# A down projection written as Strassen's seven products, in a fused mixer and SwiGLU layer

## Chip, core and metric

One Trainium2 chip, one of its cores. The metric is the device time of one execution in microseconds (us). The kernel is a whole decoder layer: four token mixers, their shared output projection, a layer norm, a SwiGLU channel mixer and a second layer norm. The change lies in the channel mixer.

## The reference

1024 tokens, model width 1024, D_FF = 2816 (22 tiles of 128), everything in float32. What bears on the change, after the mixers and the first layer norm have made x, and with sh2, sc2 and g2 the modulation of the sequence:

```python
h = x * (1 + sc2) + sh2
f = (silu(h @ w_gate) * (h @ w_up)) @ w_down
out = layer_norm(ALPHA * x + (1 + g2) * f, ln2_g, ln2_b)
```

w_gate and w_up are 1024 x 2816, w_down is 2816 x 1024.

## The kernel before

Float32 precision comes from splitting: every operand x is stored as a pair, hi = x rounded to the matmul's input type (ACT, L80) and lo = x - hi (DVE, L81), and a product is three matmuls, hi*hi, hi*lo and lo*hi (`passes`, L130 to L132). Pairs lie in tiles that go round (`pair_tile`); raw operands come by DMA into four `raw` tiles, issued by SP in program order; `tmp` is a ring of three 4 KB wide tiles. PSUM has six banks `mm` and two `sm`. The order of instructions on each engine is set by a scheduler from the order of the program, except where `in_order` holds it to program order.

**Gate and up.** For each j from 0 to 10, `strassen(j)` makes the two row tiles 2j and 2j+1 of silu(gate) * up for all tokens. It does this by five products of 24 matmuls on PE, `s1`, `s4`, `s2`, `s3` and `22`, over sums of weights that `a_ops(j)` forms (L725) and sums of activations that were formed once; two further products come from elsewhere, one loaded as `p1`. After each product DVE takes it out of PSUM, in two halves m of 128x512: L757 after `s1`, L761 after `s4`, L767 after `s2`, L774 after `s3`, L778 after `22`. `s4` goes on in the two banks that L757 reads. L781 is the multiplication by up, and L782 stores the finished tile to `act_d` in DRAM, from POOL's queue; a store at L770 writes the second half of the other tile before. `ada(38 + j)` beside it computes the modulation for the second half, and `spread(mod[40:48])` turns it into a row by a scatter through DRAM (`rowa_d`, L470).

**Down.** `down_ops` (L787) loads per row tile f a 128x512 half of act_d and the 128x1024 rows of w_down, and splits both. `down_mm` adds, for token half c, four blocks t of 128 tokens and two column halves h, the three passes into eight banks: 22 x 2 x 4 x 2 x 3 = 1056 matmuls of 128x512, 24 per row tile and half. w_down is loaded and split twice, once for each token half. The table `FB` puts the last few row tiles together so that the blocks t end one after the other, and then `res2` (L829, with L833 and L834) adds the residual to each and `ln2` (L837) normalizes it: statistics by L500 and L503, an inverse root on POOL (L397 to L415), L841, L845 and the store to the output (L846).

Of the kernel before, what the change touches and what calls it, by code (L numbers as in the profile page):

```python
# [50 lines left out]
def trunk(ctx: ExitStack, tc: tile.TileContext, A, out):  # L51
# [39 lines left out]
    def pair_tile():  # L91
        n = sum(b for _, _, b in pairs)
        i = cnt[0] % n
        cnt[0] += 1
        for pl, tg, b in pairs:
            if i < b:
                return pl.tile([P, 2, 1024], F32R, name="pr", tag=f"{tg}{i}", bufs=1)
            i -= b
# [390 lines left out]
    act_d = dr.tile([FT, P, T], F32, name="act_d")  # L489
    KORD = (6, 7, 2, 3, 0, 1, 4, 5)  # L490
# [247 lines left out]
    def strassen(j):  # L738


        ao = a_ops(j)
        w = next(ao)
# [27 lines left out]
        G.dma_start(act_d[2 * j][:, CH:], c12[0])  # L770
# [11 lines left out]
        G.dma_start(act_d[2 * j + 1], hi[0])  # L782

    FB = tuple(tuple((f, f + 1) for f in range(n)) + ((n, 22),) for n in (19, 15))
    dn = {0: {}, 1: {}}

    def down_ops(c, n):  # L787
        b0, b1 = FB[c][n]
        w, act = {}, {}
        more = sl.tile([P, 4, 2, 1024], F32R, name="wd", tag="ha") if b1 - b0 > 3 or c == 1 and n == 0 else None  # L790
        if c == 1 and n == 0:
            dn["first"] = more
        for f in range(b0, b1):
            a = raw_p.tile([P, 1024], F32, name="raw", tag="raw", bufs=4)
            SP.dma_start(a[:, :CH], act_d[f][:, cs(c)])
            act[f] = acts[(c * FT + f) % 8]
            split(act[f][:, 0], act[f][:, 1], a[:, :CH])
            if c == 1 and n < 4:
                w[f] = dn["first"][:, n]
            elif f < b1 - 3:  # L800
                w[f] = more[:, f - b0]
            else:
                w[f] = pair_tile()
            split(w[f][:, 0], w[f][:, 1], raw(A["w_down"][f]))
        dn[c][n] = w, act

    def down_mm(c, n, o):
        (b0, b1), (w, act) = FB[c][n], dn[c][n]
        for t in range(4):
            tt = slice(t * P, (t + 1) * P)  # L810
            if n == 0:
                for h in range(2):
                    o[t, h] = mm() if t < 3 else sm()
            todo = [(f, h) for f in range(b0, b1) for h in range(2)]
            if c == 1 and t == 3 and b1 == FT:
                todo.sort(key=lambda x: x[1])
            for f, h in todo:
# [11 lines left out]
    def res2(o, t, r, x1):  # L829

        for h in range(2):
            hs = slice(h * 512, (h + 1) * 512)
            V.tensor_tensor(out=r[:, hs], in0=o[t, h], in1=g2row[:, hs], op=MUL)  # L833
            V.tensor_tensor(out=r[:, hs], in0=r[:, hs], in1=x1[:, hs], op=ADD)  # L834
            yield

    def ln2(c, t, r, res=None):  # L837

        tok = c * 4 + t
        rs, nm = yield from norm_stats(r, res)  # L840
# [132 lines left out]
    with tc.issue_after(ln_end[0]), tc.issue_after(ln_end[1]), in_order(ON_PE):  # L973
# [50 lines left out]
        run(st)  # L1024
        room = sl.tile([P, 8, 1024], F32, name="room", tag="ha")
        for j in range(1, FT // 2):
            run(strassen(j))
            if j > 1 and j < 10:
                ada(38 + j)

# [4 lines left out]
    ag = row_of("ln1_g_row", sl, "m_up", ALPHA)  # L1035
    ab = row_of("ln1_b_row", sl, "m_zch", ALPHA)
    acts = hb_tiles("acts")
    o0, o1 = {}, {}
    with in_order(ON_PE):
        last = len(FB[0]) - 1  # L1040
        for n in range(last + 1):
            down_ops(0, n)
            if n == last - 1:
                x1 = [keep_x1(0, t) for t in range(4)]
            if n == last:
                for i in range(4):
                    down_ops(1, i)
            down_mm(0, n, o0)
        rr = [yp.tile([P, 1024], F32, name="r2", tag=f"y{4 + t}") for t in range(4)]
        for t in range(4):  # L1050
            run(res2(o0, t, rr[t], x1[t]))
        for n in range(len(FB[1])):
            if n > 3:
                down_ops(1, n)
            down_mm(1, n, o1)
            if 3 < n < 8:
                run(ln2(0, n - 4, rr[n - 4]))
            if n == 8:
                x1 = [keep_x1(1, t) for t in range(4)]
    rr = [tmp() for t in range(3)] + [raw_p.tile([P, 1024], F32, name="r2", tag="raw", bufs=4)]  # L1060
    ln = [ln2(1, t, rr[t], res2(o1, t, rr[t], x1[t])) for t in range(4)]
    with in_order(ON_DVE):
        for t in range(4):
            run(ln[t], 2)
            if t == 2:
# [360 lines left out]
```

## Time and profile before

| | |
|---|---|
| time, median of 3 runs (lowest to highest) | 1039.09 us (1038.07 to 1041.19) |
| the profiled execution's own time | 1037.87 us |
| its span in the trace | 1036.1 us |
| PE busy | 980.8 us, 95% |
| DVE busy | 737.7 us, 71% |
| ACT busy | 344.5 us, 33% |
| POOL busy | 184.4 us, 18% |
| moved by DMA | 177.75 MB, 172 GB/s over the span |

The page gives, for each engine, the busy time, its share of the span and the number of instructions. Busy time is an average over stages, so it says what fills the whole, and not what a stage waits for; for that the windows (busy time by stretch, with the granted clock of PE and the busy share of the DMA engines) and the timelines are read. In a timeline a row is: start, duration, engine, line and operation, output<-inputs, shape, and in square brackets the idle time of the engine just before and what ended it. PE is TensorE, DVE VectorE, ACT ScalarE, POOL GpSimd, SP SyncE. A matmul's duration in a row is longer than the distance to the next, since matmuls overlap in the pipeline.

### The profile page before, as it was taken

The page shows a single profiled execution, that of the slowest core. Times are in us where ns is not written, and L with a number is a line of the kernel's source. Part 1 is how long each engine was busy: PE and PEld are TensorE (multiplying, and loading weights), DVE is VectorE, ACT ScalarE, POOL GpSimd, SP SyncE. Part 2 cuts the span into 40 slices and gives each one's busy share as a digit, 9 for nine tenths or more (in the row PEclk, how much of TensorE's full clock was granted, in tenths as well). Part 3 has the DMA queues.
Part 4 walks back from the last instruction along what each step waited for, and adds up shares of the span by engine and source line. Part 5 has one row for each costly group of instructions (what it writes and reads, how often), then busy time and mean ns, then how long its engine had stood idle before and what let it go on. Part 6 is the DMA issues. An engine that isn't in the chain of part 4 may idle for free.

```text
span 1036.1 us, 12527 instructions
## 1 busy us (share of the span) xinstructions
PE 980.8 (95%) x4480; PEld 799.9 (77%) x4480; DVE 737.7 (71%) x1184; ACT 344.5 (33%) x537; POOL 184.4 (18%) x515
## 2 busy tenths in 40 slices
PE   8949999898989989899899999999999999999995
PEld 7837777676887868687688888887888888888884
DVE  5858998888669952757898777776568433776656
ACT  4632211424464351374322222222233333312500
POOL 7990000300351020541000000000000000050013
PEclk9979999998999999899999999999999999999998
DMA  8833212686454363597954344443247534654601
GB/s 314 321 112 104 53 41 90 219 225 223 158 204 172 147 237 104 188 316 267 347 175 159 138 147 152 146 148 111 82 149 284 174 136 142 232 185 148 228 21 61
DMA packets 65694, 177.75 MB, mean 172 GB/s; under 512 B 11040, under 2 KB 17216, under 8 KB 65632
## 3 DMA queue, kind: packets, MB, share of 16 engines
q1 hardware_dynamic: 57760, 149.17, 42.7%
q0 software_dynamic: 7872, 27.79, 6.7%
q8 instruction: 35, 0.57, 0.2%
q14 instruction: 27, 0.22, 0.1%
HBM read 142.26 MB, written 34.09 MB: 170 GB/s over the span
## 4 chain that ended last, share of the span: by engine, by line
PE 60%; DVE 10%; DMA 5%; POOL 4%; ACT 3%; issue 2%; SPq 0%; DVEq 0%; POOLq 0%; ACTq 0%
PE mm L132 18%; PE mm L130 18%; PE mm L131 17%; PE sm L130 2%; PE sm L132 2%; PE sm L131 2%; DMA raw<-in_w_ada_dram 2%; DMA raw<-h_d 2%; DVE pr L81 1%; DVE acc L429 1%; DMA raw<-in_w_gate_dram 1%; DVE raw L168 1%; ACT tmp L598 1%; DVE lst L500 1%; POOL rs_a L397 1%
## 5 line engine op out<-in xcount | busy, mean ns | idle before, releaser
L81 DVE TENSOR_TENSOR pr<-raw,pr 128x1024 fp32r<-128x1024 f32 (+1 forms) x139 | 138.1, 1003 | 77.7 <-ACT pr L80 77.4
L80 ACT CAST pr<-raw 128x1024 fp32r<-128x1024 f32 (+1 forms) x139 | 119.2, 878 | 179.4 <-PE sm L132 68.4
L130 PE MATMUL mm<-bop,pr 128*128 128x512 f32 x264 | 103.2, 391 | 4.2 <-DVE c L767 3.5
L131 PE MATMUL mm<-bop,pr 128*128 128x512 f32 x264 | 102.8, 389 | 0.0
L132 PE MATMUL mm<-bop,pr 128*128 128x512 f32 x264 | 102.7, 389 | 0.0
L130 PE MATMUL mm<-h,pr 128*128 128x512 f32 (+1 forms) x208 | 77.0, 370 | 8.0 <-ACT p L643 7.1
L429 DVE SCALAR_TENSOR_TENSOR acc<-up,pack,acc 128x512 f32<-128x512 f32 x120 | 84.3, 742 | 0.1
L130 PE MATMUL mm<-pr,acts 128*128 128x512 f32 x216 | 84.0, 389 | 0.0
L131 PE MATMUL mm<-pr,acts 128*128 128x512 f32 x216 | 84.0, 389 | 0.0
L132 PE MATMUL mm<-pr,acts 128*128 128x512 f32 x216 | 84.0, 389 | 0.0
L132 PE MATMUL mm<-h,pr 128*128 128x512 f32 (+1 forms) x208 | 75.4, 362 | 2.9 <-DVE pr L81 2.9
L131 PE MATMUL mm<-h,pr 128*128 128x512 f32 (+1 forms) x208 | 75.2, 361 | 0.0
L132 PE MATMUL mm<-tb,pr 128*128 128x512 f32 x176 | 68.8, 391 | 1.1 <-DVE pr L81 1.0
L130 PE MATMUL mm<-tb,pr 128*128 128x512 f32 x176 | 68.7, 390 | 1.0 <-ACT pr L80 1.0
L131 PE MATMUL mm<-tb,pr 128*128 128x512 f32 x176 | 68.5, 389 | 0.0
L397 POOL TENSOR_SCALAR rs_a<-lmv 128x1 f32<-128x1 f32 x16 | 11.0, 689 | 318.1 <-DVE lmv L503 317.8
L168 DVE SCALAR_TENSOR_TENSOR raw<-raw,cond 128x1024 f32<-128x1024 f32 x48 | 58.1, 1218 | 13.3 <-DMA raw<-in_w_ada_dram 13.2
L80 ACT CAST pr<-room 128x512 fp32r<-128x512 f32 x60 | 34.3, 619 | 87.9 <-PE mm L132 83.9
L130 PEld LDWEIGHTS mm<-bop,pr 128*128 128x128 f32 x264 | 49.6, 188 | 16.4 <-DVE c L767 2.9
L132 PEld LDWEIGHTS mm<-bop,pr 128*128 128x128 f32 x264 | 49.6, 188 | 10.3
L131 PEld LDWEIGHTS mm<-bop,pr 128*128 128x128 f32 x264 | 49.6, 188 | 10.1
L131 PE MATMUL mm<-h_a,pr 128*128 128x512 f32 x104 | 42.7, 410 | 13.7 <-DVE h_a L81 13.5
(311 smaller groups left out, 2182.4 us busy)
## 6 DMA issues: line engine op xcount, KB each, us to landing
raw<-in_w_ada_dram SPq DMA_DIRECT2D x48, 512.0 KB, 4.8
raw<-in_w_down_dram SPq DMA_DIRECT2D x44, 512.0 KB, 3.7
raw<-in_w_gate_dram SPq DMA_DIRECT2D x23, 512.0 KB, 4.7
raw<-in_w_up_dram SPq DMA_DIRECT2D x23, 512.0 KB, 4.2
raw<-act_d SPq DMA_DIRECT2D x44, 256.0 KB, 3.3
raw<-in_w_o_dram SPq DMA_DIRECT2D x16, 512.0 KB, 4.4
p_d<-p POOLq DMA_DIRECT2D x11, 512.0 KB, 2.9
act_d<-tmp POOLq DMA_DIRECT2D x11, 512.0 KB, 2.9
```

What stands on the lines that cost most here:

```text
L80: S.copy(hi, src)
L81: V.tensor_tensor(out=lo, in0=src, in1=hi.bitcast(F32), op=SUB)
L130: PE.matmul(o, wh, xh, start=first, stop=False, skip_group_check=True)
L131: PE.matmul(o, wh, xl, start=False, stop=False, skip_group_check=True)
L132: PE.matmul(o, wl, xh, start=False, stop=last, skip_group_check=True)
L168: V.scalar_tensor_tensor(out=w, in0=w, scalar=1.0, in1=cond, op0=MUL, op1=MUL, accum_out=mod[:, j:j + 1])
L397: G.tensor_scalar(out=a, in0=v, scalar1=EPS, scalar2=None, op0=ADD)
L429: V.scalar_tensor_tensor(out=o, in0=u, scalar=dww[:, i, j:j + 1], in1=o, op0=MUL, op1=ADD)
L500: V.bn_stats(st[:, h], r[:, h * 512:(h + 1) * 512])
L598: S.activation(dst, src, AF.Identity, scale=hA[:, kk:kk + 1], bias=hB[:, kk:kk + 1])
```

## The change

With A the activations (row tiles even or odd, tokens first or second half) and B the weights (rows even or odd, columns first or second half), the four blocks of the result are formed from seven products over 11 pairs of tiles:

1 A11 B11, 2 S1 T1, 3 S2 T2, 4 S3 T3, 5 A22 T4, 6 A12 B21, 7 S4 B22.

- The seven products run over `GR`, six groups of two tile pairs (the last has one), 24 matmuls a group, four banks `oA` or `oB` a product. The second half of the result is built up in `oA` and in SBUF (`r0`, `r1`), with copies by ACT and additions by DVE between products (`S.copy`, `res2`, `more_res`).
- S1 to S4, sums of the activations, are formed by DVE at the end of each `strassen(j)` (L788 to L792 of the change) and stored to `s_d` by POOL (two stores of 512 KB); the first half of one tile is read back for it (`c12[1]`), also from POOL's queue. The first part of the weights' sums for j+1 is issued ahead of this.
- T1 to T4, differences of the weights, are formed beside the products: `t13` makes T1 and T3 of a group during product 1, from three more loads of weights into `tmp` tiles, `t2` and `t34` turn T1 into T2 and T4 in place.
- Loads are now pieces of two tile pairs: 128 x 2 x 512, rows of 2 KB each, where w_down came in rows of 4 KB.
- Three more tiles (`m_up`, `m_zch`, `m_zp`) join the ring of pair tiles. The layer norm of the second half of the tokens ends earlier, that of the first half is now the last.

```diff
-    def strassen(j):
+    def strassen(j, ao=None, w=None):
...
-        G.dma_start(act_d[2 * j][:, CH:], c12[0])
+        G.dma_start(c12[1], act_d[2 * j][:, :CH])
...
         G.dma_start(act_d[2 * j + 1], hi[0])
+        yield
+
+        a11, a21, (a12, a22) = c12[1], c12[0], [hi[0][:, H[c]] for c in range(2)]
+        (s1, s3), (s2, s4) = P1, [hi[1][:, H[c]] for c in range(2)]
+        V.tensor_tensor(out=s1, in0=a21, in1=a22, op=ADD)
+        V.tensor_tensor(out=s2, in0=s1, in1=a11, op=SUB)
+        V.tensor_tensor(out=s3, in0=a11, in1=a21, op=SUB)
+        G.dma_start(s_d[j, 0].rearrange("p a t -> p (a t)"), p1)
+        V.tensor_tensor(out=s4, in0=a12, in1=s2, op=SUB)
+        G.dma_start(s_d[j, 1].rearrange("p a t -> p (a t)"), hi[1])
+    GR = tuple((j, min(j + 2, FT // 2)) for j in range(0, FT // 2, 2))
+    def dn_mm(o, lt, rt, g, t, first, last):
+        n = GR[g][1] - GR[g][0]
+        for j in range(n):
+            ls, rs = slice(j * CH + t * P, j * CH + (t + 1) * P), slice(j * CH, (j + 1) * CH)
+            passes(o[t], (lt[:, 0, ls], lt[:, 1, ls]), (rt[:, 0, rs], rt[:, 1, rs]),
+                   first and g == 0 and j == 0, last and g == len(GR) - 1 and j == n - 1)
+    def dn_product(o, left, right, first, last, also=lambda g: None, room=(None, None)):
+        for g in range(len(GR)):
+            lt, rt = [dn_pair(x(g), None if g else y) for x, y in zip((left, right), room)]
+            for t in range(4):
+                dn_mm(o, lt, rt, g, t, first, last)
+            also(g)
...
+        def t13(g):
+            b12, b11, b22 = (w_rows(g, b, h, tmp()) for b, h in ((0, 1), (0, 0), (1, 1)))
+            V.tensor_tensor(out=kept(g), in0=b12, in1=b11, op=SUB)
+            V.tensor_tensor(out=kept(g, True), in0=b22, in1=b12, op=SUB)
...
+        dn_product(oA, lambda g: act_rows(g, 0, 0), lambda g: w_rows(g, 0, 0), True, False, t13)
+        for t in range(4):
+            S.copy(r0[t][:, H[0]], oA[t])
+        dn_product(oB, lambda g: sum_rows(g, 0, 0), kept, True, False)
...
+        dn_product(oA, lambda g: sum_rows(g, 1, 0), t2, False, False)
...
+        dn_product(oA, lambda g: sum_rows(g, 0, 1), t34, False, False)
...
+        dn_product(oA, lambda g: act_rows(g, 1, 1), kept, False, True)
...
+        dn_product(oA, lambda g: act_rows(g, 1, 0), lambda g: w_rows(g, 1, 0), True, True,
+                   room=[more0[:, i] for i in range(2)])
...
+            ops.append((dn_pair(sum_rows(g, 1, 1), two[0]), dn_pair(w_rows(g, 1, 1), two[1])))
...
+        for t in range(4):
+            for g in range(last, len(GR)):
+                dn_mm(oB, *ops[g], g, t, False, True)
```

The scheduler puts the new work between the old. **DVE, from the end of step j=1 to the beginning of j=2, before** (L781 the multiplication of j=1, L757 the first product of j=2, L725 the weights' sums, L81 the splits; in brackets what the instruction waits for):

```order
L778 TENSOR_TENSOR tmp<-room,mm 128x512 [waits PE_49]
L81 TENSOR_TENSOR pr<-room,pr 128x512 [waits Activation_49]
L781 TENSOR_TENSOR tmp<-tmp 128x1024 [waits DVE_49]
L81 TENSOR_TENSOR pr<-room,pr 128x512 [waits Activation_49]
L757 TENSOR_TENSOR tmp<-room,mm 128x512 [waits DMAHW0_49,DMASW7_49,PE_49]
L725 TENSOR_TENSOR raw<-room,raw 128x512
L725 TENSOR_TENSOR raw<-raw,room 128x512 x2
L757 TENSOR_TENSOR tmp<-room,mm 128x512 [waits DVE_49,PE_49]
```

The same place now (L779 was L778, L782 was L781, L758 was L757; L788 to L792 are S1, S2, S3 and S4):

```order
L779 TENSOR_TENSOR tmp<-room,mm 128x512 [waits PE_49]
L81 TENSOR_TENSOR pr<-room,pr 128x512 [waits Activation_49]
L782 TENSOR_TENSOR tmp<-tmp 128x1024 [waits DVE_49]
L790 TENSOR_TENSOR room<-c_4363 128x512 [waits DMASW2_49]
L788 TENSOR_TENSOR room<-c_4363,tmp 128x512 [waits DVE_49]
L758 TENSOR_TENSOR tmp<-room,mm 128x512 [waits DMAHW0_49,DMASW1_49,PE_49]
L789 TENSOR_TENSOR tmp<-room,c_4363 128x512 [waits DVE_49]
L81 TENSOR_TENSOR pr<-room,pr 128x512 [waits Activation_49]
L792 TENSOR_TENSOR tmp<-tmp 128x512 [waits DVE_49]
L81 TENSOR_TENSOR pr<-room,pr 128x512 [waits Activation_49]
L758 TENSOR_TENSOR tmp<-room,mm 128x512 [waits DMASW3_49,DVE_49]
```

The four sums stand between the multiplication and the second L758, two of them ahead of the first; and the second L758 has a wait for a store from POOL's queue (DMASW3, the store of act_d by the step before, whose tile it writes).

**SP, the loads at the beginning of the down projection, now** (L804 is every load of the seven products; `tmp<-in_w_down_dram` are the loads for T1 and T3, `raw<-s_d` the sums for product 2):

```order
L804 DMA tmp<-in_w_down_dram 128x2x512 [waits DMASW3_49,DMASW7_49,DMASW1_49,DVE_49]
L1076 DMA keep<-in_ln_g_row_dram 128x1024 [waits DMASW4_49,DMASW0_49]
L1076 DMA keep<-in_ln_b_row_dram 128x1024
L804 DMA tmp<-in_w_down_dram 128x2x512 [waits DMAHW6_49,DMASW3_49,DMASW1_49]
L804 DMA tmp<-in_w_down_dram 128x2x512 [waits DMAHW7_49,DMAHW3_49,DVE_49]
L804 DMA raw<-in_w_down_dram 128x512 [waits DMAHW0_49,Activation_49]
L804 DMA raw<-s_d 128x2x512 [waits DMAHW1_49,Activation_49]
L804 DMA tmp<-in_w_down_dram 128x2x512 [waits DMAHW2_49,DVE_49]
L804 DMA tmp<-in_w_down_dram 128x2x512 [waits DMAHW6_49]
L804 DMA raw<-s_d 128x2x512 [waits DMAHW4_49,Activation_49]
L804 DMA raw<-s_d 128x2x512 [waits DMAHW5_49,Activation_49]
```

All of these are new; the queue held only `raw<-act_d` and `raw<-in_w_down_dram` here, in turn. Loads into `tmp` wait for DVE's subtractions and for POOL's stores, and the loads of the operands stand behind them.

## Rows read from the trace of the kernel before

**Rows 1.** The page: busy time, share of the span and instructions of each engine.

```profile
PE 980.8 (95%) x4480; PEld 799.9 (77%) x4480; DVE 737.7 (71%) x1184; ACT 344.5 (33%) x537; POOL 184.4 (18%) x515
```

**Rows 2.** Windows: length, busy PE, PEld, DVE, ACT, POOL; PE's clock, DMA share, GB/s.

```profile
785.00:965.00 180.00, 180.00 (x796) 149.10 (x795) 105.61 (x124) 53.28 (x68) 17.36 (x37) 1.00 0.53 182
508.00:540.00 32.00, 31.01 (x135) 24.83 (x134) 31.58 (x53) 12.77 (x21) 1.08 (x2) 1.00 0.64 237
785.00:797.00 12.00, 12.00 (x55) 9.94 (x54) 10.27 (x11) 3.45 (x5) 0.54 (x1) 1.00 0.97 359
830.00:860.00 30.00, 30.00 (x134) 24.86 (x133) 10.84 (x12) 8.49 (x11) 0.00 (x0) 1.00 0.39 137
595.00:622.00 27.00, 27.00 (x121) 22.37 (x120) 20.35 (x34) 7.41 (x12) 1.09 (x2) 1.00 0.41 146
434.00:438.00 4.00, 4.00 (x11) 3.13 (x10) 1.58 (x3) 3.13 (x10) 2.95 (x10) 0.50 0.32 131
```

**Rows 3.** Timeline of PE: first and last matmul of the down projection.

```profile
785.07 0.39 PE L130 MATMUL mm<-pr,acts 128*128 128x512 f32 x1
...
1024.21 0.39 PE L132 MATMUL sm<-pr,acts 128*128 128x512 f32 x1
```

**Rows 4.** Timeline of DVE at an ordinary handover between two steps.

```profile
675.17 0.69 DVE L778 TENSOR_TENSOR tmp<-room,mm 128x512 f32<-128x512 f32 x1 [1.31 <-PE mm L132]
...
680.61 0.69 DVE L757 TENSOR_TENSOR tmp<-room,mm 128x512 f32<-128x512 f32 x1 [1.72 <-PE mm L132]
```

**Rows 5.** Timelines of DVE and of PE at the first handover, j = 0 to 1.

```profile
512.70 1.22 DVE L781 TENSOR_TENSOR tmp<-tmp 128x1024 f32<-128x1024 f32 x1
513.83 0.68 DVE L81 TENSOR_TENSOR pr<-raw,pr 128x512 fp32r<-128x512 f32 x1
514.43 0.68 DVE L725 TENSOR_TENSOR raw<-raw,room 128x512 f32<-128x512 f32 x1
...
516.97 0.39 PE L130 MATMUL mm<-tb,pr 128*128 128x512 f32 x1
```

**Rows 6.** The store of act_d (L782), all steps; step 7's scatter; PE after it.

```profile
DMA to landing us min/median/max: 2.9/2.9/8.6
rowa_d<-mod SPq DMA_DIRECT2D x1, 4.0 KB, 11.1
719.69 0.47 PE L130 MATMUL mm<-bop,pr 128*128 128x512 f32 x1 [1.04 <-DVE c L767]
```

**Rows 7.** DMA issues from 783 to 800, last row 800 to 860: count, KB, us to landing.

```profile
x<-x_d SPq DMA_DIRECT2D x4, 512.0 KB, 6.3
raw<-in_w_down_dram SPq DMA_DIRECT2D x3, 512.0 KB, 4.6
act_d<-tmp POOLq DMA_DIRECT2D x1, 512.0 KB, 5.7
raw<-in_w_down_dram SPq DMA_DIRECT2D x12, 512.0 KB, 3.3
```

**Rows 8.** Groups of instructions, 785 to 1025: count, busy us, mean ns, idle before.

```profile
L81 DVE TENSOR_TENSOR pr<-raw,pr 128x1024 fp32r<-128x1024 f32 x33 | 40.3, 1220 | 51.9 <-ACT pr L80 51.8
L80 ACT CAST pr<-raw 128x1024 fp32r<-128x1024 f32 x33 | 34.7, 1052 | 64.5 <-PE sm L132 53.2 <-DMA raw<-in_w_down_dram 11.2
```

**Rows 9.** Timeline of DVE after the last matmul.

```profile
1025.17 0.68 DVE L833 TENSOR_TENSOR r<-sm,row 128x512 f32<-128x512 f32 x1
...
1027.58 1.28 DVE L841 SCALAR_TENSOR_TENSOR r<-r,lmv,row 128x1024 f32<-128x1024 f32 x1
...
1031.60 1.41 DVE L845 SCALAR_TENSOR_TENSOR r<-r,lrs,row 128x512 f32<-128x512 f32 x2 [2.73 <-POOL lrs L415]
```

**Rows 10.** Timeline of PE: two matmuls after a long pause, one after a shorter.

```profile
433.29 0.79 PE L130 MATMUL mm<-h,pr 128*128 128x512 f32 x1 [4.19 <-ACT p L643]
...
438.57 0.62 PE L130 MATMUL mm<-h,pr 128*128 128x512 f32 x1
...
501.14 0.50 PE L130 MATMUL mm<-bop,pr 128*128 128x512 f32 x1 [2.46 <-DVE c L767]
```

More of the change, by code (lines that the diff above doesn't have):

```diff
@@ L489, in trunk @@
     act_d = dr.tile([FT, P, T], F32, name="act_d")
+    s_d = dr.tile([FT // 2, 2, P, 2, CH], F32, name="s_d")
     KORD = (6, 7, 2, 3, 0, 1, 4, 5)
@@ L782, in strassen @@
         G.dma_start(act_d[2 * j + 1], hi[0])
[L784 to L805, printed above, removed]
@@ L1034, in trunk @@
     l2b = row_of("ln2_b_row", yp, "rowc")
[L1035 to L1038, printed above, removed]
+    pairs.extend((sl, f"m_{n}", 1) for n in ("up", "zch", "zp"))
     with in_order(ON_PE):
[L1040 to L1049, printed above, removed]
-        for t in range(4):
[L1051 to L1059, printed above, removed]
@@ new lines, in kept @@
+        def kept(g, third=False):
+            lo, hi = GR[g]
+            v = keep[:, 11:12] if third and lo == 10 else (kt3 if third else keep)[:, lo:hi]
+            return v.rearrange("p j t -> p (j t)")
+        ag, ab = (keep[:, 12 + 2 * i:14 + 2 * i].rearrange("p j t -> p (j t)") for i in range(2))
+        for row, name in ((ag, "ln1_g_row"), (ab, "ln1_b_row")):
+            SP.dma_start(row, A[name].to_broadcast([P, 1024]))
+            V.tensor_scalar(out=row, in0=row, scalar1=ALPHA, scalar2=None, op0=MUL)
@@ new lines, in trunk, with more_res @@
+        for t in range(4):
+            res2(r1[t], x1[t], 1, r1[t][:, H[1]])
+            run(ln1_[t], 1)
+        for t in range(4):
+            res2(r1[t], x1[t], 0, oA[t])
+        more0 = sl.tile([P, 2, 2, 1024], F32R, name="wd0", tag="hb0")
+        def more_res(t, h, o):
+            f = sl.tile([P, CH], F32, name="f", tag=f"acc{t % 2}")
+            V.tensor_tensor(out=f, in0=o, in1=g2row[:, H[h]], op=MUL)
+            V.tensor_tensor(out=r0[t][:, H[h]], in0=r0[t][:, H[h]], in1=f, op=ADD)
@@ new lines, in trunk @@
+        dn_product(oA, lambda g: act_rows(g, 1, 0), lambda g: w_rows(g, 1, 0), True, True,
+                   room=[more0[:, i] for i in range(2)])
+        for t in range(2):
+            run(ln1_[t])
+        more = sl.tile([P, 4, 2, 1024], F32R, name="wd", tag="ha")
+        last = len(GR) - 4
+        ops = []
+        for g in range(len(GR)):
+            two = (None, None) if g < len(GR) - 2 else [more[:, 2 * (g - len(GR)) + 4 + i] for i in range(2)]
+            ops.append((dn_pair(sum_rows(g, 1, 1), two[0]), dn_pair(w_rows(g, 1, 1), two[1])))
+            if g < last:
+                for t in range(4):
+                    dn_mm(oB, *ops[g], g, t, False, True)
+            if g in (1, 3):
+                run(ln1_[2 + g // 2])
@@ L1070 @@
+        run(ln0[3])
 class SSM:
```

116 lines of the change are left out of this document (79 added, 37 removed).

## The prediction

> **What bounds the kernel now.** I read the page first, then windows over the stage that is changed, then timelines of its borders, then the DMA view. The page [rows 1] shows TensorE busy for 95% of the span, every other engine below three quarters. The windows [rows 2] narrow that: from 785 to 965 us, which is three quarters of the down projection, PE is busy all the time at a granted clock of 1.00, DVE for 105.6 of 180 us, and the DMA engines for half. So the stage is paid by the matmul: its first starts at 785.07, its 1056th at 1024.21 [rows 3], which is 239.14 us over 1055 intervals, **0.2267 us each**. A matmul removed there gives that back, as long as the others find their operands in time. The gate/up stage ahead of it is also full on PE; its border between two steps j has to be looked at separately, because the change puts vector work into it.
>
> The profiled execution took 1037.87 us (span 1036.1 and 1.8 around it), 1.2 below the median of the three runs, 1039.09. My sum is against 1037.87. A difference of 0.3% (3.1 us) is about what a measurement of this kernel tells from none.
>
> **Part 1, fewer matmuls.** Seven products x 11 tile pairs x 4 row tiles x 3 passes = 924 for 1056. 132 x 0.2267 = **-29.9 us**.
>
> **Part 2, the sums S1 to S4 at the end of each strassen(j).** Four 128x512 additions go into DVE's queue among L781 and the two L757 of the next j (the two order pieces of DVE), and two more stores and a reload into POOL's. Consecutive 512-wide operations start 0.60 us apart (513.83 to 514.43) [rows 5], so four are 2.4 us. TensorE wants the first L757 done before the s4 product overwrites its bank, 24 matmuls = 5.44 us after the last product ends, and the second 2.72 later, at 8.16. At an ordinary handover [rows 4] the last product ended at about 675.15; there the second L757 starts at +5.46, after DVE has idled 1.72 us for PE, as it had 1.31 before L778. With the sums in front they are done at about +4.4 and +7.4: both in time, cost 0. Only the first handover has no slack: from 508 to 540 DVE is busy 31.58 of 32 us [rows 2], and PE's s4 product begins at 516.97 [rows 5], right after L757 ends. The four sums push the end of L757 back by all their time, 4 x 0.60, if the scheduler puts them as in the order pieces: **+2.4** (bounds 0, were DVE to catch up in the 1 us that PE lacks there, and 4).
>
> The second L757 (L758 of the change) gains a wait, for the store of act_d by the step before, because the three `tmp` buffers now go round faster. Everything behind it on DVE waits too: splits of the next operands, then PE. The store takes 2.9 us to land in most steps and 8.6 at worst [rows 6]. It is issued at +2.9; up to a landing of 4.6 us the second L757 is still done at 8.16. The worst case is step 7: the row scatter `rowa_d<-mod`, at the same place in SP's queue before and now, takes 11.1 us, and the store issued meanwhile takes the 8.6. Then L757 is done at 2.9 + 8.6 + 0.7 = 12.2 instead of 8.16, 4.0 us late, of which I take off the pause of 1.04 at 719.69 that, as I read it, the same congestion causes already [rows 6]: **+3.0** (bounds 0, if the scatter lands later, and 4).
>
> **Part 3, T1 to T4, weights' differences.** For each of six groups, product 1 also loads three weight pieces into the three `tmp` buffers, and DVE subtracts twice. SP issues in order (third order piece), so a load waiting for a buffer holds up every load behind it, those of PE's operands too. Count from T, the start of the down projection. The first of these loads needs the buffer of the last act_d store: T + 2.9 + 5.7 [rows 7] = T + 8.6; the last two need the last s_d store, about T + 11, and with the landing of 4.6 [rows 7] and two subtractions the buffers of group 0 are free at T + 19.6. From there a round takes: landing 4.6, two 1024-wide subtractions at 1.22 [rows 8] and a little, one split ahead of them, 1.13 as such operations follow each other (512.70 to 513.83) [rows 5], and 0.5 of issue by my estimate: 8.7 us. PE's round is 24 x 0.2267 = 5.44. Product 2 wants group 4 at T + 29.9 + 4 x 5.44 = T + 51.7. It is there after four rounds but for the second subtraction, and a cast and a split, T + 19.6 + 34.8 - 1.2 + 1.05 + 1.22 = T + 55.5: 3.8 late, and group 5, half as large, adds some 1.2. **+5.** Bounds: nothing, if a landing takes 3.3 us as from 800 to 860 [rows 7], for then the round is 7.4 and group 4 comes at T + 50.1, early; 13 with 6.3 us, the landing of `x<-x_d` in the crowded start [rows 7], for then a round is 10.4, group 4 comes 10.6 late and group 5 adds 2.4. I take the middle, since the stretch is fuller than 830 to 860 (137 GB/s) and emptier than 785 to 797 (359 GB/s at 0.97 share) [rows 2]: 66 pieces of 0.262 MB and two rows, about 17.8 MB, move in 59.8 us, 298 GB/s.
>
> Other work of this stretch costs nothing by itself: DVE's splits, subtractions and residuals there come by the new order to 34 operations of 1.13 and 17 of 0.60 us = 48 of 59.8 us, and ACT's casts (1.05 each [rows 8]) to less. If that cover goes, the first to suffer is the split of the T operand. The pieces are now rows of 2 KB where weights were rows of 4 KB. The rows show no price for this: 830 to 860 carries some of its bytes as 2 KB rows (activations) and moves 137 GB/s at 0.39, 351 per unit of share; 595 to 622, with 4 KB rows only, moves 146 at 0.41, 356 per unit [rows 2]. So 0 here. The Trainium skill, "Perfetto Trace Analysis", section DMA Optimizations, says the contrary, that raising transfers from 2 KB to 4 KB improves throughput; if it held, this stretch would be short of bandwidth, which is rival E. These two rows speak against it.
>
> **Part 4, the end.** Product switches on PE 0.3; operands of product 7 that fall behind the loads of the layer norm 0.7. The last four groups run row tile by row tile, 21 matmuls = 4.76 us each. DVE's work per row tile, by its spacing (2.41 from L833 to L841, then 1.28 and 1.41) [rows 9], is 5.1, a little more than PE's: it comes to end some 2 us behind PE where now L833 at 1025.17 follows the last matmul by 0.6, +1.5. The chain after that is the same length, to L845 at 1031.60 [rows 9] and the store. Together **+2.5** (bounds 0.5 and 4).
>
> **Sum.** -29.9 + 2.4 + 3.0 + 5.0 + 2.5 = -17.0: 1037.87 - 17.0 = **1020.9 us**.
>
> **Rivals.**
> B, all covered: landings stay at 3 us, the T rounds keep ahead of PE and the scatter doesn't meet the store; only the first handover is left. 1037.87 - 29.9 + 2.4 = 1010.4. For it: DVE and DMA are half idle from 785 to 965 [rows 2]. Against: both are at their fullest in products 1 and 2.
> A, the T building sets the pace: landings near 6.3, +13 instead of +5: 1029. For it: at 785 to 797 the DMA is at 0.97 already, without the extra loads [rows 2].
> D, the clock: each pause of TensorE is followed by a slow stretch. Shown once: after the pause of 4.19 before 433.29 it runs 12 matmuls at 0.427 us until 438.57, with 0.50 granted, which costs 12 x 0.2 = 2.4 us; after the 2.46 before 501.14 the first matmul takes 0.50, not 0.79, and from 508 on the clock is 1.00 [rows 2, 10]. Were four pauses in T building and one at step 7 of the first kind, +12: 1033. My pauses are 1 to 4 us long, and mostly nearer the second row. [...]
> C, **slower**: the store of act_d lands later than 4.6 us at every handover, since each step now adds a reload and two stores of 0.5 MB to the same queues; L758 then holds DVE, and PE waits up to 4.0 us at ten handovers: 1020.9 - 3 + 40 = 1058. It decides from 4.6 us on. Against: median 2.9 [rows 6], and 0.41 DMA share at those steps [rows 2].
> E, **slower**: 2 KB rows move at half the rate of the 356 GB/s per unit above, 178; 17.8 MB then take 100 us, not 59.8: +40 in place of 5, 1056. The two rows above nearly rule it out.
> That the change doesn't remove the matmuls is excluded: the order of PE has 132 rows fewer, and both print the same form.
>
> **How the numbers follow.** Forecast 0.48, A 0.22, B 0.16, D 0.08, C 0.04, E 0.02. The predicted time is the forecast's, 1020.9. The range reaches from B with the first handover free (1008) to D with a little more (1034) and leaves out C, E and the tails. Slower by over 0.3% are C and E, 0.05 after rounding; within 0.3% only a much worse A or D, 0.02; faster 0.93.
>
> **What would show it.** In the profile after: 924 matmuls at 0.227 us, no other rate; PE idle of about 2.4 us in step 1 before the s4 product, released by DVE L758; a pause of about 3 at step 8 with `act_d<-tmp` landing at 8 us or more; at 20 to 30 us into product 2 idle time of PE released by the split of `pr<-keep`, 5 us in all, with `tmp<-in_w_down_dram` landing in 4 to 5 us. PE idle at every handover would mean C; a granted clock under 1 after the pauses D; a stretch at 0.97 DMA share under 250 GB/s E; no idle in product 2 B. The prediction is wrong if PE idles outside these places, or the stage is shorter than 924 x 0.2267 = 209.5 us.

## The result, and the profile after

| | before | after |
|---|---|---|
| median (lowest to highest) | 1040.09 us (1038.07 to 1041.19, 4 runs) | 1025.55 us (1024.14 to 1029.23, 4 runs) |
| ratio to before, 95% interval | | 0.987 [0.9844, 0.9895] |
| profiled execution's own time | 1037.87 us | 1024.14 us |
| its span | 1036.1 us | 1022.4 us |

The time predicted was 1020.9, in a range from 1008 to 1034; the profiled execution fell by 13.7 us where the sum had 17.0. The page of the changed kernel, with the line of [rows 1], the chain that ended last (for it the page of before has PE at 60% and POOL at 4%), and DMA's totals:

```profile
span 1022.4 us, 12392 instructions
PE 957.6 (94%) x4348; PEld 777.6 (76%) x4348; DVE 808.0 (79%) x1268; ACT 357.3 (35%) x545; POOL 200.1 (20%) x537
issue 31%; PE 21%; DVE 12%; POOL 9%; DMA 8%; ACT 2%; SPq 0%; POOLq 0%; DVEq 0%; ACTq 0%
HBM read 153.79 MB, written 42.74 MB: 192 GB/s over the span
```

PE has 132 instructions less and 23.2 us less busy time, not the 29.9 of 132 x 0.2267, since part of its matmuls now run slower. About half of that gap lies in the down projection (below); of the rest, eight matmuls 0.43 us apart stand at 498.8 to 501.8, after a pause of 1.93 ahead of the places that the change touches. DVE is up 70 us. In the chain line 31% is "issue", time in which the engine waited for nothing that the profile shows (2% before), so the chain can be followed only in part. So the account is made from PE's own timeline, at the places where the distance between two matmuls is more than 0.2267 us:

```profile
520.42 0.50 PE L130 MATMUL mm<-tb,pr 128*128 128x512 f32 x1 [2.24 <-DVE tmp L758]
562.50 0.47 PE L130 MATMUL mm<-bop,pr 128*128 128x512 f32 x1 [0.97 <-DVE c L768]
717.48 0.47 PE L130 MATMUL mm<-tb,pr 128*128 128x512 f32 x1 [1.87 <-DVE tmp L758]
791.04 0.39 PE L130 MATMUL mm<-pr 128*128 128x512 f32 x1
821.88 0.51 PE L131 MATMUL mm<-pr 128*128 128x512 f32 x1 [0.53 <-DVE pr L81]
845.23 0.50 PE L131 MATMUL mm<-pr 128*128 128x512 f32 x1 [1.05 <-DVE pr L81]
975.98 0.59 PE L131 MATMUL mm<-pr 128*128 128x512 f32 x1 [2.15 <-DVE pr L81]
976.37 0.63 PE L132 MATMUL mm<-pr 128*128 128x512 f32 x1
1007.50 0.39 PE L132 MATMUL sm<-wd 128*128 128x512 f32 x1
```

With [rows 3] these split the difference into three parts. The down projection starts at 791.04 instead of 785.07: **+6.0**. From its first to its last matmul it takes 216.46 instead of 239.14: **-22.7**, where 923 intervals of 0.2267 would be 209.2, so 7.2 us are lost inside. From the last matmul's start to the end of the span it is 14.9 instead of 11.9: **+3.0**. 6.0 - 22.7 + 3.0 = -13.7.

The windows of the changed kernel over the stage (columns as in [rows 2]):

```profile
797.00:821.00 24.00, 24.00 (x108) 19.85 (x106) 17.84 (x19) 6.85 (x8) 0.53 (x1) 1.00 0.96 328
821.00:851.00 30.00, 28.41 (x123) 22.68 (x122) 29.04 (x31) 12.79 (x17) 0.00 (x0) 1.00 0.88 303
941.00:971.00 30.00, 30.00 (x134) 24.77 (x133) 24.50 (x34) 9.22 (x11) 14.45 (x28) 1.00 0.56 186
971.00:1007.00 36.00, 33.85 (x141) 27.14 (x140) 30.61 (x41) 8.12 (x9) 9.57 (x25) 0.95 0.35 122
```

Products 1 and 2 are the crowded ones, as forecast: DMA at 0.96, then DVE at 29.04 of 30 us. But PE loses most in the last of these windows, where DMA and POOL are little used: 2.15 us of it the pause before 975.98, and then nine matmuls 0.38 to 0.43 us apart, at a granted clock of 0.50 from 976.4 to 979.0, which cost 1.7. What ACT, DVE and POOL do there:

```profile
970.02 1.28 DVE L861 SCALAR_TENSOR_TENSOR r<-r,lmv,row 128x1024 f32<-128x1024 f32 x1
970.08 1.29 POOL L397 TENSOR_SCALAR rs_a<-lmv 128x1 f32<-128x1 f32 x1 [1.66 <-DVE lmv L858]
970.92 2.00 ACT L80 CAST pr<-raw 128x1024 fp32r<-128x1024 f32 x2 [3.44 <-PE mm L132]
974.04 0.75 DVE L865 SCALAR_TENSOR_TENSOR r<-r,lrs,row 128x512 f32<-128x512 f32 x1 [2.73 <-POOL lrs L415]
974.71 2.35 DVE L81 TENSOR_TENSOR pr<-raw,pr 128x1024 fp32r<-128x1024 f32 x2
```

L861 is done at 971.3; DVE then stands for 2.73 us at L865, the last step of a layer norm, until POOL has the inverse root, and behind L865 in its queue stand the two splits (L81) of the operands that PE wants for product 7. From 971.30 to 974.04 DVE does nothing, and POOL runs the nine tiny instructions of one root. The first of the two splits did not wait for its operand: ACT's casts of both are done by 972.9, that of the first by 971.9.

The end of the kernel, POOL and DVE:

```profile
1002.63 0.76 POOL L397 TENSOR_SCALAR rs_a<-lmv 128x1 f32<-128x1 f32 x1
...
1003.91 1.28 DVE L861 SCALAR_TENSOR_TENSOR r<-r,lmv,row 128x1024 f32<-128x1024 f32 x1
...
1004.15 1.26 POOL L402 TENSOR_SCALAR rs_b<-lrs,rs_a 128x1 f32<-128x1 f32 x1
...
1006.95 0.34 POOL L402 TENSOR_SCALAR rs_b<-lrs,rs_a 128x1 f32<-128x1 f32 x1
...
1007.93 0.76 POOL L397 TENSOR_SCALAR rs_a<-lmv 128x1 f32<-128x1 f32 x1
...
1010.40 0.68 DVE L1121 TENSOR_TENSOR f<-sm,row 128x512 f32<-128x512 f32 x1
...
1013.22 0.76 POOL L397 TENSOR_SCALAR rs_a<-lmv 128x1 f32<-128x1 f32 x1
...
1017.94 1.41 DVE L865 SCALAR_TENSOR_TENSOR r<-r,lrs,row 128x512 f32<-128x512 f32 x2 [2.16 <-POOL lrs L415]
```

POOL begins a root every 5.29 us (1002.63, 1007.93, 1013.22), with no idle between two, while PE delivers a row tile every 4.76. Before, a root that met DVE only at its first instruction took 4.0, from 1027.64 to L845 at 1031.60 [rows 9]. DVE reaches the last row tile (L1121) at 1010.40, 2.5 us after the last matmul's end, where before it was 0.6.

### The profile page after: what moved, and what is told of

It is laid out like the page before. It is cut to its first block, busy times and chain, and to the rows that moved or that the text cites. A ratio compares the mean times of both kernels' runs of the same rounds, so it can differ in the third digit from the quotient of the medians.

```text
span 1022.4 us, 12392 instructions
## 1 busy us (share of the span) xinstructions
PE 957.6 (94%) x4348; PEld 777.6 (76%) x4348; DVE 808.0 (79%) x1268; ACT 357.3 (35%) x545; POOL 200.1 (20%) x537
## 4 chain that ended last, share of the span: by engine, by line
issue 31%; PE 21%; DVE 12%; POOL 9%; DMA 8%; ACT 2%; SPq 0%; POOLq 0%; DVEq 0%; ACTq 0%
PE mm L132 6%; PE mm L130 6%; PE mm L131 6%; DVE pr L81 3%; DMA raw<-in_w_ada_dram 2%; DMA tmp<-in_w_down_dram 2%; POOL rs_b L402 2%; DVE acc L429 1%; POOL rs_a L397 1%; DVE raw L168 1%; ACT tmp L599 1%; DMA raw<-h_d 1%; POOL rs_b L409 1%; DMA tmp<-x_d 1%; DMA raw<-s_d 1%
## 5 line engine op out<-in xcount | busy, mean ns | idle before, releaser
L80 ACT CAST pr<-raw 128x1024 fp32r<-128x1024 f32 (+1 forms) x157 | 133.6, 876 | 180.4 <-PE mm L132 53.9
L81 DVE TENSOR_TENSOR pr<-raw,pr 128x1024 fp32r<-128x1024 f32 (+1 forms) x157 | 155.4, 1002 | 31.0 <-ACT pr L80 30.6
L131 PE MATMUL mm<-pr 128*128 128x512 f32 x250 | 98.6, 394 | 3.9 <-DVE pr L81 3.7
L132 PE MATMUL mm<-pr 128*128 128x512 f32 x250 | 98.2, 393 | 0.0
L130 PE MATMUL mm<-pr 128*128 128x512 f32 x250 | 98.1, 392 | 0.0
L397 POOL TENSOR_SCALAR rs_a<-lmv 128x1 f32<-128x1 f32 x16 | 8.7, 546 | 292.8 <-DVE lmv L858 179.4
L131 PEld LDWEIGHTS mm<-pr 128*128 128x128 f32 x250 | 47.4, 189 | 15.8 <-DVE pr L81 6.1
```

The source lines that it names most:

```text
L80: S.copy(hi, src)
L81: V.tensor_tensor(out=lo, in0=src, in1=hi.bitcast(F32), op=SUB)
L130: PE.matmul(o, wh, xh, start=first, stop=False, skip_group_check=True)
L131: PE.matmul(o, wh, xl, start=False, stop=False, skip_group_check=True)
L132: PE.matmul(o, wl, xh, start=False, stop=last, skip_group_check=True)
L397: G.tensor_scalar(out=a, in0=v, scalar1=EPS, scalar2=None, op0=ADD)
```

## The experiments

The kernel before measured 1039.0 to 1044.0 us in the four groups of runs that are compared below, so the ratios are what to compare; the change has 0.987. Most effects are a few us, near what separates two runs of one kernel, so each verdict rests on the pauses and the tail in the trace as well.

**e1: the second half's layer norm later in the program**

```diff
-        for t in range(2):
-            run(ln1_[t])
...
-            if g in (1, 3):
-                run(ln1_[2 + g // 2])
+            if 1 <= g <= 4:
+                run(ln1_[g - 1])
```

> The layer norm of the second token half (its four row tiles, in the changed kernel two before product 7 and two inside it) is put into product 7 behind its first operands. Theory (DVE's queue): the pause of 2.15 us before product 7 and the nine slow matmuls after it come from splits that stand behind L865, which waits for POOL's inverse root; with the layer norm behind the splits the pause and the slow matmuls go: about 4 us faster than the change, 1021 to 1022 us. Rival (loads): the operands of product 7 come late because their loads stand behind stores of the output in SP's queue; then the order on DVE alone brings under 1 us and the pause at the border stays.

1028.22 us, ratio 0.9884 [0.9848, 0.9921]. DVE before product 7 in e1:

```profile
973.23 1.28 DVE L861 SCALAR_TENSOR_TENSOR r<-r,lmv,row 128x1024 f32<-128x1024 f32 x1
977.25 0.75 DVE L865 SCALAR_TENSOR_TENSOR r<-r,lrs,row 128x512 f32<-128x512 f32 x1 [2.73 <-POOL lrs L415]
977.91 2.35 DVE L81 TENSOR_TENSOR pr<-raw,pr 128x1024 fp32r<-128x1024 f32 x2
```

The same queue with the same wait: the scheduler put the layer norm in the same place, wherever the program had it. So e1 is inconclusive; the pause stayed at 2.16, and e3 and e6 ask the question again.

**e2: longer row tiles at the end**

```diff
-        last = len(GR) - 4
+        last = len(GR) - 5
```

> The last five groups instead of four run row tile by row tile, so each row tile takes 27 matmuls (6.1 us) instead of 21 (4.76 us). Nothing else moves. Theory (POOL): the tail is set by the inverse root, 5.3 us of POOL for each row tile, back to back; at 6.1 us it keeps up, and from the last matmul to the end it takes 12 us, as before the change, not 14.9: 2 to 3 us faster than the change. Rival (a lag of DVE that is already there when the tail begins): the tail stays at 14 or more.

1029.37 us, 0.9905 [0.9875, 0.9934]. The tail did what the theory said: last matmul at 1015.12, span 1027.0, 11.9 us instead of 14.9. But the kernel is no faster: there are two new pauses of 2.2 and 1.0 us at 990.6 and 992.1, the second with eight slow matmuls behind it, and the old one before product 7 stays (2.13). PE now needs the operands of five groups within the first row tile, and they are late; why is asked by e7 and e10. A gain in one place, paid for in another.

**e3: a shorter root**

```diff
-        for cubic in (True, False):
+        for cubic in both:
...
-        rsqrt(rs, mv[:, 1:2])
+        rsqrt(rs, mv[:, 1:2], (True,))
```

> Leaves out the second refinement (three small POOL instructions) of the inverse root in the last layer norm; DVE's work is the same. Theory (POOL sets the tail): a row tile's root falls from 5.3 to about 4.1 us, below the 4.76 us of PE, so the tail shortens by 1.1 for the last root and by 1.5 to 2.5 for the queue before it: 2.5 to 3.5 us in all, from 14.9 to about 12. Rival (DVE, 5.0 us per row tile, sets it): only the last root is shorter, 1.1 us.

**1018.70 us, 0.9805 [0.9772, 0.9837]**, the largest gain of all, and its interval lies below that of the change: faster, from twelve instructions less on [128 x 1] in the tail and twelve in product 6. This kernel leaves the second refinement of the root out, so it is a probe and no replacement. POOL in its tail:

```profile
1003.45 0.59 POOL L397 TENSOR_SCALAR rs_a<-lmv 128x1 f32<-128x1 f32 x1 [0.74 <-DVE lmv L858]
...
1008.22 0.59 POOL L397 TENSOR_SCALAR rs_a<-lmv 128x1 f32<-128x1 f32 x1 [0.74 <-DVE lmv L858]
```

A root every 4.77 us, PE's pace, and POOL waits for DVE, not DVE for POOL. The tail is 11.95 (last matmul 1004.25, span 1016.2), 3.0 less, inside the theory's 2.5 to 3.5 and not the rival's 1.1. And what was not expected of this run: the pause before product 7 is gone as well. The window from 971 to 995 in e3:

```profile
971.00:995.00 24.00, 24.00 (x107) 19.44 (x106) 22.29 (x29) 8.21 (x9) 0.00 (x0) 1.00 0.46 154
```

PE is busy for all 24.00 us at full clock, with DVE's work the same. By place, product 7 loses 0.3 us where the change loses 4.4, and the tail is 2.9 shorter (14.86 to 11.95); elsewhere little moves. So both losses have one cause: POOL's chain of small instructions.

**e4: the sums of step 0 later**

```diff
-            run(st)
-            st = strassen(j, ao, w)
-            run(st, 5)
+            prev, st = st, strassen(j, ao, w)
+            run(st, 2 if j == 1 else 0)
+            run(prev)
+            run(st, 3 if j == 1 else 5)
```

> At the first handover alone, the four sums of step 0 come behind the first two products of step 1; all other steps are as in the change. Theory: the 2.24 us pause of PE at 520.4, released by L758, is the four sums in DVE's queue; it goes, 2.4 us faster than the change. Rival: DVE is full there, so the sums only push something later; PE pauses within the next 20 us and the time stays within 1 us of the change.

1024.59 us, 0.9863 [0.9815, 0.9911]. PE at the first handover, and DVE before it:

```profile
520.53 0.68 DVE L758 TENSOR_TENSOR tmp<-room,mm 128x512 f32<-128x512 f32 x1
521.36 0.47 PE L130 MATMUL mm<-tb,pr 128*128 128x512 f32 x1 [1.47 <-DVE tmp L758]
```

The first L758 is ahead of the sums now (515.67), but the second still has all four in front: it writes a tile of the ring of three `tmp` that the sums read. So the pause shrinks from 2.24 to 1.47, and the one at 562.50 (0.97 in the change) goes with it: 1.7 us of the forecast 2.4 on the trace, and less than the runs can tell apart. That second pause hangs on the sums as well: it is there in the eight traces that keep this place as in the change and the three tiles (0.3 to 1.1 us), and in none of the four with e4's edit. By the time, within 1 us of the change, and by a pause that stays, this is the rival's side.

**e5: more buffers**

```diff
-        hi = [tmp() for _ in range(2)]
+        hi = [tmp(), tmp() if j == 0 else far_tile(j)]
...
-            b12, b11, b22 = (w_rows(g, b, h, tmp()) for b, h in ((0, 1), (0, 0), (1, 1)))
+            b12, b11, b22 = (w_rows(g, b, h, far_tile(g) if b else tmp()) for b, h in ((0, 1), (0, 0), (1, 1)))
```

> Two idle tiles (y4, y5) take one of the two tiles of every strassen step from the second on, and in products 1 and 2 two of the three weight pieces for T1 and T3, so that the ring of three tmp tiles is shared by fewer. The order of the program is the same otherwise. Theory (the ring of tmp): the second L758 no longer waits for a store of the step before, so the pause of 2 to 3 us at 715 to 718 goes, and T is built one group ahead, so that the pauses in products 1 to 3 (2.2 in the change, 1.7 to 3.6 in the four runs above) fall under 1 us: 3 to 5 us faster than the change. Rival (bandwidth): the loads are late because the DMA engines are full; then the pauses in products 1 to 3 stay above 1.5 us. The first handover (2.4) and the pause before product 7 stay by both.

(The diff is what ran: of the three pieces one, not two, went to the other tiles.) **1042.52 us, 1.0012 [0.9988, 1.0036]**: the whole gain of the change is gone. In the gate/up stage DVE's wait for `room<-in_w_gate_dram` (from 520 to 800 us) rises from 13.8 to 27.1 us. At step 8 L758 no longer waits for the store, but PE waits 3.37 us at 734.66, with DVE waiting for a load of w_gate that was issued late. Two subtractions for T1 in the change (L1080) and the two at the same groups in e5 (L1083):

```profile
825.15 1.22 DVE L1080 TENSOR_TENSOR keep<-tmp 128x1024 f32<-128x1024 f32 x1
833.17 1.22 DVE L1080 TENSOR_TENSOR keep<-tmp 128x1024 f32<-128x1024 f32 x1
830.89 1.23 DVE L1083 TENSOR_TENSOR keep<-tmp 128x1024 f32<-128x1024 f32 x1 [1.18 <-DMA tmp<-in_w_down_dram]
836.58 1.22 DVE L1083 TENSOR_TENSOR keep<-tmp 128x1024 f32<-128x1024 f32 x1
```

At the start of the down projection SP, ACT and PE of e5 read:

```profile
826.70 5.81 SPq L807 DMA_DIRECT2D tmp<-in_w_down_dram  x2
832.56 0.46 SPq L807 DMA_DIRECT2D raw<-s_d  x1
837.18 1.04 ACT L80 CAST pr<-raw 128x1024 fp32r<-128x1024 f32 x1 [6.48 <-DMA raw<-s_d]
838.28 0.79 PE L130 MATMUL mm<-pr 128*128 128x512 f32 x1 [6.82 <-ACT pr L80]
```

The rounds of T are shorter, 6.4, 5.7 and 5.7 us for the change's 8.0, and no pause is left at group 4 of product 2, with DMA at 0.90 from 821 to 851. So the ring did set the round, as the theory said. What took the gain is the order in SP's queue: the loads for T stand ahead of the first `raw<-s_d`, the operand of product 2, which is issued at 832.56 where the change has it at 809.25, and PE stands 6.82 us. By its outcome, pauses over 1.5 us, this is the rival's side, but not by its reason: the ring held T back, and at the same time kept the loads in a good order.

**e6, e7 and e10: the layer norm spread over product 6, and the end**

The edit of e6 (order() puts L865 behind the latest split; e7 adds e2's line; e10 adds to e7 the early splits):

```diff
+            if c == 1:
+                order(i.ins, dn["split"].name)
...
+            run(ln1_[t], 1)
...
+                   also=lambda g: 1 <= g <= 4 and run(ln1_[g - 1]),
```

> The layer norm of the second token half stands in another place: the four statistics and inverse roots are issued before product 6, and the two instructions that wait for a root (L865) are held, one row tile a group, behind the splits of groups 1 to 4 of product 6. No work is left out. Theory (DVE stands behind POOL): PE's pause of 2.15 before product 7 and the slow matmuls after it go, about 4 us faster than the change; the tail from the last matmul stays at 14.8. Rival (the operands of product 7 are late for another reason, their loads or the pair tiles): the pause stays over 1 us.

1027.37 us, 0.9862 [0.9822, 0.9903]. The pause of 2.15 is gone, as the theory said: with the layer norm moved and nothing left out of it, the pause goes, so it hung on the layer norm's place in DVE's queue, which agrees with e3's edit of the root. Of the gain the runs show none, though the interval doesn't exclude it: 1.0 us of pause appears at 991.78, inside product 7, two of 0.2 at 950, and more matmuls run at the lower clock after the old pauses at 501 and 719. Products 6 and 7 lose 2.7 us where the change lost 4.4. The tail is 14.9, as expected.

> The edit of e6_norm_spread, and five groups instead of four row tile by row tile at the end, as in e2_tail27. Theory: both gains add, the pause before product 7 gone (4 us) and the tail 12 instead of 14.8 (3 us): 7 us faster than the change, if the two pauses of 2.2 and 1.0 near 991 of e2_tail27 came from the loads that the output's stores held up in SP's queue. Rival: those two pauses came from the pair tiles that five groups hold at once; then they stay and the second gain is lost, as it was there.

1031.79 us, 0.9894 [0.9860, 0.9929]. The tail is 11.9; pauses of 2.5 and 1.1 at 993.6 and 995.5 stayed. The rival's side by the outcome; that the pair tiles are the reason is not shown by it.

```diff
+        def early(g):
+            ready[g] = (dn_pair(sum_rows(g, 1, 1), more[:, 2 * g - 8]), dn_pair(w_rows(g, 1, 1), more[:, 2 * g - 7]))
...
+            ops.append(ready.get(g) or (dn_pair(sum_rows(g, 1, 1)), dn_pair(w_rows(g, 1, 1))))
```

> As e7_spread_tail27, and the operands of product 7's last two groups are loaded and split during product 6, into tiles that are free by then. Theory (in e7 the operands of five groups could not be made in the time of one row tile, 6.1 us): the pauses near 990 us (2.5 and 1.1 in e7, 1.2 in e6) go, none stays at the border before product 7, and the tail is 12 us: PE loses under 1 us from 940 us to its last matmul, and the kernel is 6 to 7 us faster than the change, about 1019. Rival (product 6 is then too full on DVE): pauses of the same size in product 6.

1030.60 us, 0.9890 [0.9859, 0.9920]. Tail 11.9 again; the pauses moved forward, to 977 to 993, 5.5 us in five. What ACT and SP of e10 waited for from 960 to 1000 (total, times, longest):

```profile
ACT pr L80 <- DMA raw<-in_w_down_dram: 18.7, 6, 9.7
...
SPq L804 <- DVE pr L81: 9.7, 8, 2.4
SPq L871 <- DVE r L868: 6.7, 6, 2.1
```

The casts wait for loads, and the loads stand in SP's queue for two reasons: they wait for the splits (L81) that free the `raw` tiles, 9.7 us, and they stand behind stores of the output (L871) that wait for L868 and by it for POOL's root, 6.7 us. For the pause at 981.5 (2.06) the late load is issued at 975.43, right behind such stores; for those at 991 to 993 the loads, from 982.74 on, wait for splits alone. So e10 speaks against the pair tiles as the reason in e7. Which of the two waits makes the operands late is open: no run separates them. Two of the five pauses lie in product 6 or at its border, where the rival had them.

**e8: e4, e5 and e7 together**

> All four edits: the spread layer norm, five groups at the end, the late sums at the first handover, and the two tiles more. Theory: the pauses are independent, so 4 + 3 + 2.5 + 4 us come off the change: 1012 to 1014 us, and PE loses under 5 us between 510 us and its last matmul. Rival: a pause that is filled only moves to the next scarce thing (DVE, then DMA): 1018 or more.

1040.09 us, 0.9978 [0.9953, 1.0003]: the rival's side by the time, with e5's loss as the largest part, a pause of 7.0 us at 835.1.

**e9: T3 formed later**

```diff
-            V.tensor_tensor(out=kept(g, True), in0=b22, in1=b12, op=SUB)
+        def t3(g):
+            b11 = w_rows(g, 0, 0, tmp())
+            V.tensor_tensor(out=kept(g, True), in0=kept(g), in1=b11, op=SUB)
```

> T3 is formed during product 3 as T2 - B11 from one load, no longer during product 1 as B22 - B12; T1 stays. The number of loads and subtractions is the same in all, but product 1's groups load two pieces for T instead of three, and subtract once instead of twice. Theory (loads of T stand in SP's queue ahead of the operands, while the DMA engines are at 0.9 or more): the pauses between 815 and 865 us (2.2 in the change, 1.7 to 3.6 in other runs) fall under 1 us, and the DMA share from 797 to 821 falls from 0.96 to about 0.8; 2 us faster. Rival (the start of the stage, where the first loads for T wait for the stores of the last step): the first pause, at the border of products 1 and 2, stays.

1029.02 us, 0.9871 [0.9844, 0.9898], the change's ratio. DMA from 797 to 821 falls only to 0.90. With one piece less to load for each group the rounds of T1 fall to 5.3 to 6.4 us and the pause at group 4 goes, as in e5; but pauses at 819.6 and 824.4 (0.5 and 1.7) stand at the first border, as the rival had it, and a new one of 1.05 at 886.2, where product 4 begins, which uses the T3 that is now formed in product 3.

**e11: e4, e9 and e10 together**

> The edits of e4, e9 and e10 together. Theory: the pauses they take away lie in different places (first handover, products 1 to 3, products 6 and 7 and the end), so the gains add: 2 + 2 + 6.5 us off the change, about 1015. Rival: the sums that are late at the first handover and the layer norm in product 6 each push other work; less than half of it, 1020 or more.

1030.23 us, 0.9882 [0.9851, 0.9913]. The first handover (1.47, none at 562) and the tail (11.9) are as in the single runs, and product 7 loses the 5 us of e10. The rival's side.

**e12: the root in seven instructions, nothing left out, and e4**

```diff
-        rsqrt(rs, mv[:, 1:2])
...
+        G.tensor_scalar(out=b, in0=rs, scalar1=rs, scalar2=a, op0=MUL, op1=MUL)
+        G.tensor_scalar(out=b, in0=b, scalar1=-10 / 3, scalar2=b, op0=ADD, op1=MUL)
+        G.tensor_scalar(out=rs, in0=b, scalar1=5.0, scalar2=rs, op0=ADD, op1=MUL)
+        G.tensor_scalar(out=b, in0=rs, scalar1=rs, scalar2=a, op0=MUL, op1=MUL)
+        G.tensor_scalar(out=rs, in0=b, scalar1=-64 / 3, scalar2=rs, op0=ADD, op1=MUL)
...
-    l2g = row_of("ln2_g_row", yp, "rowb")
+    l2g = row_of("ln2_g_row", yp, "rowb", -0.0263671875)
```

> Nothing is left out: the inverse root of the last layer norm in seven POOL instructions instead of nine, with the same two refinements (their constant factors are put into the row ln2_g, which is scaled once when it is loaded), and the sums of step 0 at the late place of e4_sums_late. Theory (POOL's chain delays DVE before product 7 and sets the end): most of the gain of e3_short_root comes back, since 7 instructions are near its 6: the pause before product 7 and the slow matmuls after it go (4 us), the tail is about 12.5 us instead of 14.9, and with 2 us from the first handover the kernel is 7 to 8 us faster than the change: a ratio to the kernel before of 0.980 or a little less, where the change has 0.987. Rival (what counts is a refinement less, below PE's 4.76 us per row tile, and one instruction more than in e3 is too many): the tail stays above 13.5 and the pause above 1 us, ratio 0.985.

**1023.92 us, 0.9822 [0.9781, 0.9862]**, the lowest ratio of a kernel that computes all; its interval touches that of the change, so that it is faster than the change is likely, not shown. On the trace the pause before product 7 is 0.63 without slow matmuls behind it, but one of 0.94 is new at 990.91, so product 7 loses 2.6 us (the change 4.4, e3 0.3); the tail is 13.4 (last matmul 1008.52, span 1021.9). That is half of e3's effect on the tail, and less than half of it at product 7. POOL's roots follow each other at 4.94 us, still without idle, a little over PE's 4.76. Both sides of the expectation were partly right.

## Why the prediction was right, and where its steps were not

The range and the sign held, and the sum was 3.3 us too favourable. That it fits so well is luck in part. The losses were forecast as 12.9 us and measured as 16.2, but place by place they are 2.4 for 2.4 at the first handover, 0.8 for 3.0 at step 7, 2.9 for 5.0 in the building of T, 7.4 for 2.5 at the end, and 2.7 at places that had no term: terms that were too large and one that was too small nearly cancel. By its own sign of being wrong the prediction failed in part: PE idles at places that it doesn't name (562.50, 975.98), and nine matmuls ran at 0.38 to 0.43 us where it had said "no other rate".

- **132 x 0.2267 = -29.9: right.** Where nothing is late, the matmuls run at the same distance: 502 intervals from 859.61 to 973.44 us, 0.2268 us each.
- **First handover, +2.4: right**, 2.40 by the distance from 517.79 to 520.42 less 0.2267, and 2.4 in each run that kept the sums there. Moving them took a third of it (e4). That it is right to the tenth is in part luck. DVE's rows, the first of the kernel before, the other two of the change:

```profile
515.64 0.68 DVE L757 TENSOR_TENSOR tmp<-room,mm 128x512 f32<-128x512 f32 x1
513.74 1.21 DVE L782 TENSOR_TENSOR tmp<-tmp 128x1024 f32<-128x1024 f32 x1
519.70 1.27 DVE L758 TENSOR_TENSOR tmp<-room,mm 128x512 f32<-128x512 f32 x2
```

  From the multiplication (512.70 before [rows 5], 513.74 now) to this operation it is 3.0 us longer, the four sums and one other operation more; and the s4 product began 0.65 after the end of L757 before, a slack that I had put at none. 3.0 less 0.65 is 2.4. What I missed is that the sums cost PE once more, a step later, in the pause before 562.50 (see e4).
- **Step 7, +3.0: the mechanism right, the size not.** The second L758 waited for the store of act_d, as said:

```profile
716.65 0.69 DVE L758 TENSOR_TENSOR tmp<-room,mm 128x512 f32<-128x512 f32 x1 [2.31 <-DMA act_d<-tmp]
```

  The store took 6.2 us to land, not 8.6; why it lands sooner now is not shown. PE lost 2.0 less the 1.2 that were there before, 0.8. That is one trace: the eleven with this code give 0.8 to 3.4, 2.0 in the mean.
- **T, +5: the mechanism right, 2.9 measured**, 2.4 in product 2 and 0.5 in product 3. The subtractions for T1 in the changed kernel start at 816.99, 825.15, 833.17 and 841.08, rounds of 8.0 us for my 8.7, and the pause, at the split of `pr<-keep`, is at group 4 of product 2 (845.23), where the sum had it. That the ring sets this round is borne out by e5 and e9, whose rounds are shorter. The size is near the low end: the nine traces with this code lose 2.8 to 6.5 in products 2 and 3, 4.4 in the mean, so they don't show +5 to be wrong.
- **The end, +2.5: the step that was wrong**, 7.4 measured. It costed DVE's work by row tile and took POOL's root from a row where it met DVE only at its first instruction; the 0.3 for product switches and the 0.7 for late operands stood on no row. DVE's lag behind PE grew by 1.9, near the 1.5 of the sum, but not for its reason: in e3, with DVE's work the same, the lag is 1.1 us at the same place, not 2.5. With a row tile every 4.76 us a root takes 5.29 of POOL, and the chain behind the last row tile is 1.1 longer too: +3.0 in the tail. At product 7 the same root, in front of splits in DVE's queue, cost 2.3 of pause and 1.7 of slow clock, 4.0 for 0.7. e3 shows that both are the root's; e6 (the order before product 7) and e2, e7 and e10 (longer row tiles) show it by other edits, each for one of the two.
- Rest: 1.0 us of the later start was there before step 0's handover (PE at 515.61, 514.57 before), at a place that the change doesn't touch; in nine of the twelve other runs that matmul starts between 513.6 and 516.1. 1.5 lies in step 2, with the pause at 562.50.
- **Rivals.** A did not come: landings were 4.5 in the median. B would have needed T and the end to be free. C did not come, the store landed in 2.9 in the median and no other handover has a pause. E is small: 328 GB/s at 0.96 share is 342 per unit, against 370 in the crowded window of before [rows 2], so the crowded stretch moves some 8% less per share of busy engines, far from half; that 2 KB rows are the cause was not tried. The Trainium skill, "Perfetto Trace Analysis", section DMA Optimizations, says that larger pieces improve throughput: these 8% go that way, but no run shows that the rows cause them. D came once in the down projection: the lower clock took 1.7 us after the pause of 2.15.
- Two small slips of the prediction's sums change nothing: its 66 pieces and two rows are 18.3 MB, 307 GB/s, and C and E together have a chance of 0.06.

## What to carry to other kernels

When a matmul stage gets shorter, look for the chains that had its length as cover, on the engines with the lowest busy share too: here nine instructions on 128 numbers, on an engine that is busy for 20%, cost 7 of the 30 us won. A value that one engine makes and another waits for costs everything queued behind the waiter, so shorten that chain before adding buffers. And more buffers are not always safer: in e5 they let loads that nobody waited for yet go ahead of those that PE needed, and the whole gain was gone.

## What the runs showed of the hardware

- **Small POOL instructions stretch beside DVE.** L402 takes 0.34 us at 1006.95, and 1.26 at 1004.15, where DVE runs L861 from 1003.91 to 1005.19: it ends just after that. L398 takes 0.19 alone and 0.56 beside L865, L409 0.26 and 0.79 beside L1122. Beside L1121, which reads PSUM, there is no such stretch. A root takes 3.9 us where it meets DVE only at its first instruction (970.08 to 974.01), 5.2 in the tail (1002.63 to 1007.84) and 6.0 in product 6 (956.35 to 962.34). Why was not tried.
- **The clock after a pause.** In the fourteen traces, from 490 us on, pauses of 0.2 to 1.9 us were followed by matmuls at 1.2 GHz in 7 of 119 cases, each within 3 us behind another pause; the rest kept 2.4. After the pauses of 2.13 to 2.16 before product 7, seven to nine matmuls ran at about 0.43 us (clock 0.50 in the change from 976.4 to 979.0) in five runs of six, and none in e1. After those of 2.21 to 2.26 at the first handover some did in four runs of nine. What decides it is open.
